# Moving four of the adaLN vectors from TensorE to VectorE, spread over four feed-forwards

## The chip, the core and the metric

One core of one Trainium2 chip runs the whole program in one launch. The time is device microseconds of that core, the median of three runs. A profile is one more execution; the rows below come from it.

## The reference, cut to what matters

Two blocks of layers run one after the other on 256 tokens of width 1024, beside 256 context tokens. Every layer is conditioned: a vector `c` (and another one for the context) is passed through Silu and multiplied by a weight matrix, and the product, plus a bias, is cut into vectors of 1024 that shift, scale and gate what the layer does.

```python
silu_c, silu_cc = silu(c), silu(c_ctx)
for i in range(2):                                  # first block
    mod_lat = (silu_c  @ mod_w[i] + mod_b[i])       # 9 vectors of 1024
    mod_ctx = (silu_cc @ mod_w[i] + mod_b[i])       # used by layer 0 alone
    ...
for i in range(2):                                  # second block
    sh1, sc1, g1, sh2, sc2, g2 = split(silu_c2 @ mod_w2[i] + mod_b2[i], 6)
    csh1, csc1, ... = split(silu_cc2 @ mod_w2[i] + mod_b2[i], 6)   # layer 0: the first two are used
    ...
```

There are 30 such vectors, each a product with a 1024 x 1024 piece of weights (4 MB in fp32). Vectors 0 to 4 of the first layer and 0 and 1 of the second block's first layer are wanted for both the tokens (keys `l00`..., `r00`...) and the context (`c0`..., `d0`...); all others for the tokens alone.

## The kernel before, in words

Everything is fp32 in feature-major tiles. A weight tile of 128 x 1024 is loaded raw (`wraw`, 512 KB, 3 buffers), cast by ScalarE to a high part (`wh`, L287) and split by VectorE into a low part (`wl`, L288; 6 buffers of each), and PE does three products for every pair (`mm3`).

The program runs: filters for the last mixer (`hyena_filters`), the joint feed-forward of tokens and context (`ffn_two`, 69.5 to 461 us of the span), attention (to 640), the feed-forwards `half_ffn(0,1)` and `half_ffn(1,0)`, a Fourier mixer, `half_ffn(1,1)`, the recurrent mixers (`ab_mixer`), the feed-forward `w130`, the Hyena mixer, the feed-forward `w131`. `ffn_two` has two halves; each makes 11 blocks of the up-projection (48 matmuls of 512 columns, a gate of ScalarE and VectorE) and then 8 pieces of the down-projection (33 matmuls).

The vectors are made in the background, in two ways. `mod_param` (L154) is PE's: for each of four `k` it loads a `modw` tile of 1 MB and multiplies it with the conditioning columns, 4 matmuls of 32 columns (8 instructions in the trace), for both rows at once; then ScalarE copies, PE transposes four times, VectorE adds the bias. That is five steps for a vector. `mod_vector` (L189) is VectorE's: for each of eight `c` it loads a `modx` tile of 512 KB (3 buffers) and reduces it against the broadcast row `crow` (L205). With two keys, each step has two more reductions of half the width for the second row (L201 to L204); no vector takes that path before. `VEC` (L63) says which vectors are VectorE's: 23 of 30, all those with one key. PE has seven.

Two generators, `fill` (PE's) and `fillv` (VectorE's), walk through the vectors in order; `pump(n)` and `pump_v(n)` trace their next `n` steps at a place in the program. `ffn_two` asks for `fillers[half]` steps of PE and `fillers[2]` of VectorE behind a block, and `fillers[3]` of VectorE behind a piece of the down-projection; the other feed-forwards take theirs from `self.ff`. `need(keys)` (L259) pumps until the keys are there. A scheduler then orders the instructions of each engine: of those that are ready by its reckoning, the earliest in the program goes first, so a step can run well ahead of its place in the text. Engines and queues work through that order strictly. Both ways take their tiles from one pool, `modp`, on `mstack`; SP's queue issues the loads of weights, `modw` and `modx`; POOL's queue loads `crow`.

In the filters 13 steps of PE's generator are asked for, which makes two vectors and three of the four products of the third.

```python
VEC = {"mw0": (5,6,7,8), "mw1": tuple(range(9)), "nw0": (2,3,4,5), "nw1": tuple(range(6))}
...
                self.pump(fillers[half])
                if j < HB - 1:
                    self.pump_v(fillers[2])
```

Of the kernel before, what the change touches and what calls it, by code (L numbers as in the profile page):

```python
# [19 lines left out]
KC = D // P  # L20
# [39 lines left out]
    return np.ascontiguousarray(w.reshape(2, 4, P, n, T).transpose(3, 0, 2, 1, 4))  # L60


VEC = {"mw0": (5,6,7,8), "mw1": tuple(range(9)), "nw0": (2,3,4,5), "nw1": tuple(range(6))}  # L63


def mod_tiles(w, vec):

    n = w.shape[1] // D
    t = w.reshape(KC, P, n, D).transpose(2, 0, 1, 3).copy()
    for j in vec:  # L70
        t[j] = w[:, j * D:j * D + D].T.reshape(KC, P, D)
    return t
# [6 lines left out]
class Gen:  # L79
    def __init__(self, tc, a, o):  # L80
        self.tc = tc
        self.nc = tc.nc
        self.a = a
        self.o = o
        self.n = 0
        self.hold, self.busy = False, set()
        self.ff = ((0,0,1,2),(0,0,1,2))
        self.gaps = (1,2,2)
        self.bg = []

# [139 lines left out]
    def filler(self, vec):  # L230
        for n, i, j, keys in self.mods():
            if (j in VEC[f"{n}w{i}"]) != vec:
                continue
# [23 lines left out]
            next(self.fillv, None)  # L257

    def need(self, *keys):  # L259
        while any(k not in self.prm for k in keys):  # L260
            self.pump(1)
            self.pump_v(1)


    def split(self, raw, shape, tag, pool=None, bufs=None):
# [306 lines left out]
            for x, *_ in todo:  # L572
                nc.scalar.activation(out=x[:, c, :], in_=x[:, c, :], func=AF.Copy, scale=ALPHA)

    def ffn_two(self, wi, wo, H, ahead, first, done, pool, fillers=(1,1,1,2)):

        hh, hl = lambda c: H[0][:, :, c, :], lambda c: H[1][:, :, c, :]
        for half in range(2):
            dh = pool.tile([P, HB, 2, T], F32R, tag="dh", name=self.nm("dh"), bufs=1)
            dl = pool.tile([P, HB, 2, T], F32R, tag="dl", name=self.nm("dl"), bufs=1)  # L580
            for j in range(HB):
                blk = ahead.pop() if ahead else [self.weights(wi[half * HB + j, x]) for x in range(2)]
                (pa, pg), = self.up_group([blk], hh, hl, 2 * T)
                self.glu(pa, pg, dh[:, j], dl[:, j], [P, 2, T], pool)
# [3 lines that stand above are left out]
            for f in range(KC):  # L588
                ps = self.po.tile([P, 2, T], F32, tag="out", name=self.nm("dn"))
                for c0 in (0, 8):  # L590
                    n = min(8, HB - c0)
                    wh, wl = self.weights(wo[f, :, half * HB + c0:half * HB + c0 + n, :])
                    for j in range(n):
                        self.mm3(ps, wh[:, j, :], wl[:, j, :], dh[:, c0 + j], dl[:, c0 + j],
                                 c0 + j == 0, c0 + j == HB - 1)
                (done if half else first)(f, ps)
                self.pump_v(fillers[3])


    def rope(self, dst, src, pool):  # L600
# [1149 lines left out]
    def build(self):  # L1750
        nc, tc, a, prm = self.nc, self.tc, self.a, self.prm
        pool = lambda n: tc.tile_pool(name=n, bufs=1, reuse_waits="tile")
        self.cols = self.cp.tile(list(a["cols"].shape), F32, tag="cols", name="cols")
        i = 0
# [8 lines left out]
        H = [h[:, :, 0:KC * T].rearrange("p n (c t) -> p n c t", c=KC) for h in Hr]  # L1763
# [5 lines left out]
        def post(l, j, X, s, sc, sh, out, alpha, tag="a"):  # L1769
            g, b = LG(l, j)  # L1770
            mod = None
            if sc is not None:
                self.need(sc, sh)
                mod = self.affine(g, b, sc, sh, tag)
            self.layer_norm(X, s, g, b, mod, out and out[0], out and out[1], alpha)
# [6 lines left out]
        def into(gate, n, l, sc, sh):  # L1782


            self.need(gate, sc, sh)
            s = self.acc_begin(False)
            r = []

            def done(f, ps):
                self.gated(X, prm[gate], s, f, ps)  # L1790
                if f == 1:
                    r.append(self.raw_begin(*R0, *self.affine(NW(n, l), None, sc, sh, "a")))
                    self.raw_chunk(r[0], X, 0)
                if f:
                    self.raw_chunk(r[0], X, f)

            def end():
                self.rms_norm(X, s, r[0].g2, r[0].sh, *H1, raw=r[0])
                return r[0]
            return done, end  # L1800
# [12 lines left out]
        ahead = []  # L1813
        with pool("hf") as p:
# [5 lines left out]
                    ahead.append([self.weights(a["wi00"][0, x]) for x in range(2)])  # L1820
            self.hyena_filters(kf, H, X, hook, p)

        with pool("f0") as p:
            while "c1" not in prm:
                self.pump(1)
            self.modulate([(X, "l01", "l00", *H0), (Xc, "c1", "c0", *H1)])
            sl, sc = self.acc_begin(True), self.acc_begin(True)

            def first(f, ps):
                self.need("l02", "c2")  # L1830
                for x, k, i in ((X, "l02", 0), (Xc, "c2", 1)):
                    nc.vector.scalar_tensor_tensor(out=x[:, f, :], in0=ps[:, i], scalar=prm[k][:, f:f + 1],
                                                   in1=x[:, f, :], op0=ALU.mult, op1=ALU.add)

            def second(f, ps):
                self.gated(Xc, prm["c2"], sc, f, ps[:, 1])
                self.gated(X, prm["l02"], sl, f, ps[:, 0])
            self.ffn_two(a["wi00"], a["wo00"], H, ahead, first, second, p)
            post(0, 0, Xc, sc, "c4", "c3", H1, None, "c")
            post(0, 0, X, sl, "l04", "l03", H0, ALPHA)  # L1840
# [42 lines left out]
        done, end = into("r02", "norm2", 0, "r04", "r03")  # L1883
        self.project(a["ab_wo"], *H1, done, early)
        raw = end()
        done, end = into("r05", "norm1", 1, "r11", "r10")
# [4 lines left out]
        done, end = into("r12", "norm2", 1, "r14", "r13")  # L1891
# [142 lines left out]
def host_inputs(v):  # L2034
# [7 lines left out]
    for i in range(2):  # L2042
        r[f"mw{i}"], r[f"nw{i}"] = mod_tiles(f("mod_w")[i], VEC[f"mw{i}"]), mod_tiles(f("mod_w_2")[i], VEC[f"nw{i}"])
        for k in range(2):
# [36 lines left out]
```

## Time and profile before

| | |
|---|---|
| median of the runs | 2132.93 us (2126.7 to 2133.91) |
| the profiled execution | 2130.68 us, span 2128.9 us |
| PE busy | 2023.3 us, 95% of the span |
| VectorE (DVE) busy | 1437.3 us, 68% |
| ScalarE (ACT) busy | 958.9 us, 45% |
| mean granted TensorE clock | 0.967 |
| HBM read | 400.78 MB, 191 GB/s over the span |

PE's busy time counts overlapping matmuls and weight loads as work and is no measure of how close PE is to its peak. The start of one matmul to the start of the next is the better measure of its pace. In the first fifth of the span the DMA engines move over 300 GB/s; after that less.

### The profile page before, as it was taken

How to read it: one execution, taken by the hardware profiler on the slowest of the kernel's cores; microseconds unless marked ns; L12 is line 12 of the kernel's file. 1: busy time of each engine (PE TensorE's matmuls, PEld its weight loads, DVE VectorE, ACT ScalarE, POOL GpSimd, SP SyncE). 2: the span in 40 equal slices, each digit the busy share in tenths (PEclk: the TensorE clock that was granted, in tenths of full speed). 3: DMA queues.
4: the chain of work that ended last, by engine and by line, in shares of the span. 5: the costliest groups of instructions: out<-in, count | busy, mean ns of one | idle time of the engine just before them, and what ended most of it. 6: DMA issues, size and time to landing. Idle time of an engine off the chain costs nothing.

```text
span 2128.9 us, 39134 instructions
## 1 busy us (share of the span) xinstructions
PE 2023.3 (95%) x15750; PEld 1848.4 (87%) x15750; DVE 1437.3 (68%) x2654; ACT 958.9 (45%) x1651; POOL 203.2 (10%) x240
## 2 busy tenths in 40 slices
PE   7999999977699999999999999989989999999998
PEld 3677877767579999999999997978879998999998
DVE  6766876899966555655565646686788757887553
ACT  3622222235656445544554436344354545445442
POOL 1000000150020001001120021211020001001001
PEclk9999999988899999999999998999989999999999
DMA  9988998886524664666346553222158865525663
GB/s 322 341 314 307 328 323 311 287 291 222 163 70 149 186 186 144 198 191 201 114 131 194 163 158 92 70 67 81 52 179 296 261 190 184 168 87 174 192 185 107
DMA packets 115885, 408.56 MB, mean 192 GB/s; under 512 B 13492, under 2 KB 16244, under 8 KB 115320
## 3 DMA queue, kind: packets, MB, share of 16 engines
q1 hardware_dynamic: 111480, 391.86, 56.4%
q0 software_dynamic: 4224, 14.21, 2.0%
q8 instruction: 123, 2.02, 0.4%
q14 instruction: 58, 0.48, 0.1%
HBM read 400.78 MB, written 5.24 MB: 191 GB/s over the span
## 4 chain that ended last, share of the span: by engine, by line
PE 67%; issue 18%; DVE 9%; DMA 3%; ACT 2%; POOL 1%; SPq 0%; POOLq 0%; DVEq 0%; ACTq 0%
PE up L293 30%; PE dn L293 14%; PE pfm L293 3%; PE pj L293 3%; PE ptm L293 3%; PE phu L293 2%; DVE modx L205 2%; DVE wl L288 2%; PE phs L293 1%; PE st L293 1%; PE phy L293 1%; PE phk L293 1%; ACT wh L287 1%; PE pu L293 1%; PE psk L293 1%
## 5 line engine op out<-in xcount | busy, mean ns | idle before, releaser
L288 DVE TENSOR_TENSOR wl<-wraw,wh 128x1024 fp32r<-128x1024 f32 (+1 forms) x511 | 611.4, 1198 | 397.4 <-ACT wh L287 396.6
L293 PE MATMUL up<-H,wh 128*128 128x256 f32 (+2 forms) x4224 | 858.2, 302 | 3.2 <-ACT H L499 3.2
L287 ACT CAST wh<-wraw 128x1024 fp32r<-128x1024 f32 (+1 forms) x511 | 517.7, 1014 | 713.3 <-PE up L293 334.5
L293 PEld LDWEIGHTS up<-H,wh 128*128 128x128 f32 x4224 | 679.8, 190 | 45.4 <-ACT silu L331 13.4
L293 PE MATMUL up<-H,wl 128*128 128x256 f32 (+2 forms) x2112 | 636.1, 301 | 2.8 <-DVE wl L288 2.8
L293 PEld LDWEIGHTS up<-H,wl 128*128 128x128 f32 x2112 | 405.9, 192 | 19.4 <-DVE wl L288 3.0
L293 PE MATMUL dn<-dl,wh 128*128 128x256 f32 (+1 forms) x1056 | 317.5, 301 | 0.6 <-DVE dl L335 0.6
L293 PE MATMUL dn<-dh,wh 128*128 128x256 f32 (+1 forms) x1056 | 317.7, 301 | 0.0
L293 PE MATMUL dn<-dh,wl 128*128 128x256 f32 (+1 forms) x1056 | 317.4, 301 | 0.0
L205 DVE CUSTOM_DVE_ANT_0 modx<-modx,crow 128x1024 f32<-128x1024 f32 x184 | 229.9, 1268 | 92.6 <-DMA modx<-i_mw 79.8
L293 PEld LDWEIGHTS dn<-dh,wh 128*128 128x128 f32 x1056 | 199.0, 188 | 8.8 <-issue 0.8
L293 PEld LDWEIGHTS dn<-dl,wh 128*128 128x128 f32 x1056 | 198.9, 188 | 8.7 <-DVE dl L335 1.1
L293 PEld LDWEIGHTS dn<-dh,wl 128*128 128x128 f32 x1056 | 199.0, 188 | 7.6
L293 PE MATMUL pj<-H,wh 128*128 128x256 f32 x480 | 86.5, 281 | 0.4 <-ACT H L473 0.3
L412 POOL TENSOR_TENSOR accQ<-accQ,sq 128x256 f32<-128x256 f32 x55 | 73.2, 1331 | 88.7 <-ACT sq L402 87.2
L334 ACT CAST dh<-gluh 128x256 fp32r<-128x256 f32 (+1 forms) x128 | 56.4, 443 | 47.6 <-DVE gluh L333 46.8
L293 PE MATMUL phu<-H,wh 128*128 128x256 f32 (+1 forms) x384 | 73.2, 288 | 3.4 <-ACT H L542 1.4
L293 PE MATMUL pfm<-H,wh 128*128 128x256 f32 (+1 forms) x288 | 74.0, 339 | 2.4 <-ACT t L1325 1.3
L293 PEld LDWEIGHTS pj<-H,wh 128*128 128x128 f32 x480 | 74.1, 188 | 1.3 <-ACT H L473 0.5
L293 PE MATMUL ptm<-wh,H 128*128 128x256 f32 x384 | 72.7, 291 | 0.0
L293 PE MATMUL pj<-H,wl 128*128 128x256 f32 x240 | 67.6, 282 | 1.8 <-DVE wl L288 1.8
L293 PEld LDWEIGHTS phu<-H,wh 128*128 128x128 f32 x384 | 60.9, 193 | 4.9 <-ACT H L542 1.8
(477 smaller groups left out, 2620.3 us busy)
## 6 DMA issues: line engine op xcount, KB each, us to landing
wraw<-i_wi SPq DMA_DIRECT2D x176, 512.0 KB, 4.5
wraw<-i_w SPq DMA_DIRECT2D x120, 512.0 KB, 4.2
modx<-i_mw SPq DMA_DIRECT2D x104, 512.0 KB, 5.8
modx<-i_nw SPq DMA_DIRECT2D x80, 512.0 KB, 4.8
wraw<-i_wo SPq DMA_DIRECT2D x64, 512.0 KB, 4.3
modw<-i_mw SPq DMA_DIRECT2D x20, 1024.0 KB, 8.0
wraw<-i_hy_in SPq DMA_DIRECT2D x24, 512.0 KB, 4.5
wraw<-i_wo SPq DMA_DIRECT2D x24, 384.0 KB, 3.8
```

Source lines behind the costliest of these rows:

```text
L205: nc.vector.tensor_tensor_reduce(out=ws[c - 1], in0=ws[c - 1], in1=rows[0], scale=1.0, scalar=0.0, op0=ALU.mult, op1=ALU.add, accum_out=ts ...
L287: nc.scalar.copy(out=hi[:, :f], in_=raw[:, :f])
L288: nc.vector.tensor_tensor(out=lo[:, :f], in0=raw[:, :f], in1=hi[:, :f].bitcast(F32), op=ALU.subtract)
L293: return self.nc.tensor.matmul(out, lhsT=l, rhs=r, start=start, stop=stop, skip_group_check=True, **kw)
L334: nc.scalar.copy(out=dh, in_=h)
L412: nc.gpsimd.tensor_tensor(out=s.Q, in0=s.Q, in1=sq, op=ALU.add)
```

## The change

`VEC` gives VectorE vectors 3 and 4 of the first layer and vectors 0 and 1 of the second block's first layer as well; all four have two keys. PE keeps vectors 0, 1 and 2 of the first layer. VectorE's steps rise from 184 to 216, PE's products fall from 28 to 12. Ahead of the joint feed-forward the program finishes PE's third vector, closes `modp` and opens it again, so that PE's 16 KB of `modw` buffers in each partition are given up and the rows `crow` are loaded anew. `ffn_two` asks for no PE steps, for 4 VectorE steps behind a block (1 before) and 3 behind a piece of the down-projection (2 before), none behind the last two pieces. The three feed-forwards of the first block ask for 1.3 steps a block (28 for 22). `need` pumps only the generator to which the missing key belongs.

```diff
-VEC = {"mw0": (5,6,7,8), "mw1": tuple(range(9)), "nw0": (2,3,4,5), "nw1": tuple(range(6))}
+VEC = {"mw0": (3,4,5,6,7,8), "mw1": tuple(range(9)), "nw0": tuple(range(6)), "nw1": tuple(range(6))}
...
-        self.ff = ((0,0,1,2),(0,0,1,2))
+        self.ff = ((0,0,1.3,2),(0,0,1,2))
...
     def need(self, *keys):
-        while any(k not in self.prm for k in keys):
-            self.pump(1)
-            self.pump_v(1)
+        for k in keys:
+            vec = any(k in ks and j in VEC[f"{n}w{i}"] for n, i, j, ks in self.mods())
+            while k not in self.prm:
+                self.pump_v(1) if vec else self.pump(1)
...
-    def ffn_two(self, wi, wo, H, ahead, first, done, pool, fillers=(1,1,1,2)):
+    def ffn_two(self, wi, wo, H, ahead, first, done, pool, fillers=(0,0,4,3)):
...
-                self.pump_v(fillers[3])
+                if half == 0 or f < KC - 2:
+                    self.pump_v(fillers[3])
...
+        self.need("c0", "c1", "c2")
+        self.mstack.close()
+        self.open_m()
         with pool("f0") as p:
-            while "c1" not in prm:
-                self.pump(1)
...
             def first(f, ps):
-                self.need("l02", "c2")
```

## Rows read from the trace of the kernel before

**Rows 1.** Busy times by stage: us, then PE, PEld, DVE, ACT, POOL; clock, DMA share, GB/s.
```profile
258.00:385.00 127.00, 127.00 (x579) 96.18 (x577) 88.75 (x154) 31.28 (x43) 0.00 (x0) 1.00 0.87 312
461.00:640.00 179.00, 136.42 (x944) 115.44 (x944) 152.00 (x379) 99.41 (x201) 20.33 (x22) 0.85 0.51 163
...
1595.00:1713.00 118.00, 117.97 (x988) 117.97 (x989) 90.36 (x134) 58.59 (x88) 0.00 (x0) 0.99 0.82 269
```
**Rows 2.** Groups by shape, 69.5 to 461 us: VectorE's reductions and PE's products.
```profile
L205 DVE CUSTOM_DVE_ANT_0 modx<-modx,crow 128x1024 f32<-128x1024 f32 x128 | 162.0, 1289 | 84.4 <-DMA modx<-i_mw 79.8 <-ACT crow L221 3.6 <-DMA modx<-i_nw 0.5
...
L293 PE MATMUL mod<-modw,cond 128*32 128x512 f32 x136 | 18.1, 605 | 0.0
```
**Rows 3.** Waits, 69.5 to 461 us: total us, times, longest.
```profile
ACT wh L287 <- PE up L293: 152.3, 18, 9.4
DVE modx L205 <- DMA modx<-i_mw: 79.8, 29, 5.7
```
**Rows 4.** Timeline of PE in the first block: start, us.
```profile
69.31 0.63 PE L293 MATMUL up<-H,wh 128*128 128x512 f32 x2
...
70.00 0.63 PE L293 MATMUL up<-H,wh 128*128 128x512 f32 x2
```
**Rows 5.** Timeline of ScalarE: the Silu at the end of three blocks.
```profile
153.33 0.59 ACT L331 ACTIVATE silu<-up 128x512 f32<-128x512 f32 x1
...
164.86 0.59 ACT L331 ACTIVATE silu<-up 128x512 f32<-128x512 f32 x1
...
177.14 0.59 ACT L331 ACTIVATE silu<-up 128x512 f32<-128x512 f32 x1
```
**Rows 6.** Timeline of VectorE, a reduction and the split behind it.
```profile
406.15 1.22 DVE L205 CUSTOM_DVE_ANT_0 modx<-modx,crow 128x1024 f32<-128x1024 f32 x1
...
407.30 1.22 DVE L288 TENSOR_TENSOR wl<-wraw,wh 128x1024 fp32r<-128x1024 f32 x1
```
**Rows 7.** Timeline of VectorE in the attention: two reductions of 512.
```profile
591.90 0.69 DVE L673 CUSTOM_DVE_ANT_0 sc<-pss,band 128x512 f32<-128x512 f32 x1
...
592.51 0.69 DVE L673 CUSTOM_DVE_ANT_0 sc<-pss,band 128x512 f32<-128x512 f32 x1
```
**Rows 8.** The tiles modw and modx: issues on SP's queue, ns min/median/max, first and last start.
```profile
L163 SPq DMA_DIRECT2D modw<-i_nw x8: 378/382/387, 191.4 to 360.6; - x8
...
L198 SPq DMA_DIRECT2D modx<-i_mw x104: 327/328/1052, 65.8 to 390.0; - x104
```
**Rows 9.** Timeline of VectorE: the first reduction; the second block's splits.
```profile
75.32 1.23 DVE L205 CUSTOM_DVE_ANT_0 modx<-modx,crow 128x1024 f32<-128x1024 f32 x1 [3.02 <-DMA modx<-i_mw]
...
78.93 2.52 DVE L288 TENSOR_TENSOR wl<-wraw,wh 128x1024 fp32r<-128x1024 f32 x2 [0.22 <-ACT wh L287]
```
**Rows 10.** Busy times and granted clock at the start of the attention.
```profile
493.00:496.00 3.00, 3.00 (x8) 2.32 (x8) 3.00 (x9) 2.32 (x5) 0.00 (x0) 0.50 0.94 370
```
**Rows 11.** Groups of VectorE by shape, 421 to 458 us.
```profile
L205 DVE CUSTOM_DVE_ANT_0 modx<-modx,crow 128x1024 f32<-128x1024 f32 x14 | 23.5, 1716 | 0.0
```
**Rows 12.** Timeline of PE behind the last down-projection.
```profile
464.19 1.02 PE L293 MATMUL st<-onem,Xc 128*128 128x1 f32 x4 [3.89 <-DVE Xc L548]
```
**Rows 13.** The tile modx by stretch: us, VectorE busy and count; clock, DMA share, GB/s.
```profile
397.00:461.00 64.00, 35.70 (x24) 1.00 0.87 295
...
520.00:640.00 120.00, 18.81 (x16) 0.91 0.42 135
640.00:835.00 195.00, 0.00 (x0) 0.98 0.59 177
...
1600.00:1713.00 113.00, 23.06 (x19) 1.00 0.83 273
```
**Rows 14.** Busy times in the attention behind the last reduction.
```profile
590.00:613.00 23.00, 20.12 (x138) 13.54 (x136) 15.03 (x46) 16.62 (x43) 0.00 (x0) 0.93 0.00 1
```
**Rows 15.** The chain behind the recurrent mixers: two updates of X.
```profile
1565.88 0.47 DVE X L548
...
1569.51 0.40 DVE X L548
```

## The prediction

> **What bounds the kernel now.** I read the busy times by stage first, then groups, waits and the timeline. The change acts in the joint feed-forward, from 69.5 to 461 us. There PE is busy without a gap at full clock, in the second up-projection for 127.00 of 127 us, while VectorE fills 88.75; from 461 to 640, in the attention, PE has gaps and VectorE is busy 152 of 179 us [rows 1]. So PE sets the pace up to 461 and VectorE is close behind; after it VectorE is nearest to the bound.
>
> Next the groups of that stretch: the matmuls on 32 columns for the vectors (mod), and 128 reductions (modx) at 1289 ns [rows 2]. The program text asks for 52 reduction steps in this stage; 128 ran. So steps are pulled forward from later feed-forwards into whatever time is free: the order of the program is a priority, not a place. The list of waits says that ScalarE's casts wait 152.3 us for PE to release a weight buffer, so the splits run as far ahead as the buffers let them, and that VectorE waits 79.8 us for modx loads without PE noticing [rows 3].
>
> **PE's relief.** Two pairs of matmuls of the up-projection follow each other by 0.69 us with one matmul between, so 0.231 us each and 48 x 0.231 = 11.1 us for a block [rows 4]. The Silu of the blocks starts at 153.33, 164.86 and 177.14: a block with four transposes takes 11.53 us, one with a product of a vector 12.28 [rows 5]. One product costs 12.28 - 11.1 = 1.17 us of PE, a set of transposes 0.43. Of 17 products in this stage (136 instructions by 8) [rows 2] 16 go (four vectors by four) and four sets of transposes: 16 x 1.17 + 4 x 0.43 = **-20.5 us**, all of it on PE, which is the bound. The ends are 0, if VectorE or the loads take over, and 20.5.
>
> **What moves to VectorE.** Four vectors of eight steps, all with two results, one for each conditioning row. A step has a 1024-wide reduction, 1.15 us from start to start [rows 6], and two 512-wide ones. No 512-wide modx ran; the nearest is the 512-wide reduction of the attention, 0.61 us from start to start, its other source in PSUM [rows 7]. So 1.15 + 2 x 0.61 = 2.37 us a step; 32 steps are 76 us of VectorE, against 20.5 us of PE. Below 0.58 (half the 1.15) and above 0.69 (its whole duration) I see no reason to go: 2.31 to 2.53.
>
> The bytes are the same, 16 loads of 1 MB for 32 of 512 KB. SP's queue issues 32 x 0.33 for 16 x 0.38 us [rows 8], 4.5 us more over 370; it waits for buffers most of that time, so I put nothing. In the trace loads of 512 KB are the rule already, and the last down-projection, which has no 1 MB loads, moved its weights and 24 steps in 64 us, at 0.87 of the DMA engines' time [rows 13]. The Trainium skill, page "DMA: Bandwidth & Descriptors", section "Rules for kernel authors", speaks against it: it wants 1 MiB in each transfer for full bandwidth. [...]
>
> **Early delay.** The first two vectors in VectorE's order (3 and 4 of the first layer) are of the two-result kind, though their results are wanted only at 460. Four steps are now asked for behind each block and so stand ahead of the splits of the next block. VectorE's load for a block is then 4 x 2.37 + 2 splits of 1.2 [rows 6] + 2 instructions of 0.61 for the gate, put at the 512-wide price above, = 13.1 us, and PE takes 11.1. Before, the first reduction ran at 75.32 and the second block's splits ended at 81.4 [rows 9]. With the pool closed and opened again, the rows loaded again and PE's third vector finished first, I put the first step at 82 (an estimate between 75 and 90). Before the fourth block's splits stand 12 steps, three gates and the splits: 82 + 28.4 + 3.7 + 2.4 = 116.5, while PE wants them at 81.4 + 2 x 11.1 = 103.6: 12.9 us late, and 2.0 more for the next block. Splits that slip in while a load is on its way take some of it off; a rest of that size also costs PE its clock: after its idle time from 459 on PE was granted 0.50 still at 493 to 496 [rows 10]. I take **+13 us**. The ends are 0 (all splits slip in) and +20 (none does, loads late, 5 us at half clock).
>
> **Late delay.** The next two-result vectors are steps 121 to 136. Before, the 128 steps up to 461 came out even; without the 1 MB loads step 121 comes at about the end of the second up-projection. So 16 two-result steps lie in the last down-projection, beside POOL's sums. There a reduction takes 1716 ns instead of 1.22 us, a factor of 1.40 [rows 6, 11], and VectorE ends 3.89 us behind PE [rows 12]. Before, 24 reductions lay there [rows 13]: 24 x 1.72 = 41 us. Now 16 x 2.37 x 1.40 = 53 us, 12 more on a full engine; if only the wide reduction is slowed, 16 x (1.15 x 1.40 + 1.22) = 45 and 4 more. The Trainium skill, "GPSIMD Engine Reference", section "Specifications", has VectorE contend with POOL in instructions with two SBUF inputs; the halves are such, so by that page it would be +12. I take **+6 us**, the splits being some blocks ahead; ends 0 and +12.
>
> **The rest of the work.** 216 steps instead of 184, 140 or so done at 461 instead of 128, so some 75 are left instead of 32 before the mixers, and 24 less after them. The attention took in 32, the last 16 of them after 520, and from 640 to 835 there is none [rows 13]: the supply had run out. Now it goes on. From 590 to 613 VectorE has 8 of 23 us free [rows 14]; at the pace before, 16 in 120 us or denser, five to eight more steps of 1.15 us come in there and in the norm at 640, part of them on the chain: **+5 us**, ends 0 (all in gaps) and +12 (each on the chain, and waits for loads of about 4 us). In the three feed-forwards behind, 30 steps fit beside a PE-bound up-projection: 19 steps between 1600 and 1713 left PE full, 117.97 of 118 us [rows 1, 13]; I put +1 for the start, ends 0 and 3. The closing of the pool itself moves the third vector's last product ahead of the modulation, 1 MB in front of the first blocks' weights: **+1**, ends -2 and +4. The extra memory is used by nothing.
>
> Behind the mixers nothing is left to reduce. The chain there runs through VectorE, and the updates of X come 3.63 us apart with reductions and a row's Silu between them [rows 15], where PE needs 24 matmuls of half the columns of an up-projection's, 24 x 0.116 = 2.8 us [rows 4]; six updates at 0.8 are 4.8, which I round down for what the weights hold up: **-4 us**, ends 0 and -6. The wait on the running vector ahead of the mixers costs nothing, before or after: it had long run.
>
> **Sum.** -20.5 + 13 + 6 + 5 + 1 + 1 - 4 = +1.5 us against the profiled execution's 2130.7 (span 2128.9 and 1.8 around it), which lies 2.2 below the median 2132.9. For the median: 2134.4, said as 2134. A change under 0.3%, 6.4 us, can't be told from none here.
>
> **Rivals.** *The relief wins.* If the splits keep slipping in during the first blocks, as they did before when all reductions were of lower priority, the early and late delays are some 4 and 2 us: -20.5 + 4 + 2 + 3 + 1 - 4 = -15, 2118. For it: VectorE's 79.8 us of waiting for modx loads are free time in which PE missed nothing [rows 3]. Against it: the free time lies inside an in-order queue, and the steps now stand first. *VectorE becomes the bound.* The place is the queue of VectorE between 82 and 130 and again from 400 to 461: if no split slips in and POOL slows the halves too, +20 + 12 + 6 + 1 + 1 - 20.5 - 3 = +16, 2149. It decides when the delay in the first four blocks is over 15 us. For it: 13.1 us of load against 11.1 a block; against it: buffers of three blocks. *It doesn't do what it says.* Since steps are pulled forward anyway, the new counts in the feed-forwards may move hardly anything, and only PE's four vectors count; then the two-result steps are gap-fillers and it ends near the first rival, 2116. [...]
>
> **Numbers.** Forecast 0.35; relief wins, with the case of idle counts, 0.30; VectorE bound 0.32; transfers 0.03. The forecast's own range is 2127 to 2139, the bounds of "same" about the median. 8 times in 10: from 2113, the relief with a lower price in the attention, to 2156, VectorE bound with a dearer attention. Faster 0.30, same 0.35, slower 0.35.
>
> **What would show it.** Right: no mod matmul after about 80 us; blocks of 11.1 us; PE idle for 10 us or more between 100 and 135, released by wl; reductions at 3 us a step in the last down-projection; modx instructions between 590 and 835; none after 1550. Wrong: no PE wait in the first four blocks (then it is faster by 10 to 20), or a wait on wraw loads, or the up-projections of the later feed-forwards longer than 128 us.

## The result, and the profile after

The changed kernel takes 2157.52 us (median of four runs, 2154.83 to 2160.77) against 2130.13 for the kernel before beside it (2126.7 to 2133.91): a ratio of 1.0124, 95% interval 1.0108 to 1.0140. That is 23 us above the forecast of 2134 and just above the range. The profiled span is 2156.5 us.

Where the 27 us arise is read from PE's timeline: the start of the first matmul of each stage. The table gives the kernel before in us and how much later each kernel gets there; the runs are explained below. Each column is one profiled execution, and that can lie off the median of its runs: by -4.5 us for before_slot, and by +9.4 us for two_moved, which is not in the table.

| stage starts | before | after | own_scratch | loads_alone | finish_first | before_slot | slot_4late |
|---|---|---|---|---|---|---|---|
| joint feed-forward | 63.7 | +12.6 | +11.9 | +13.5 | +15.1 | +0.9 | -0.2 |
| its second block | 81.0 | +9.3 | +8.5 | +10.3 | +15.7 | +4.7 | -0.2 |
| first down-projection | 202.3 | +17.1 | -1.8 | +18.1 | +14.5 | +8.8 | -0.2 |
| second down-projection | 396.5 | +9.0 | -7.7 | +11.1 | +13.0 | +8.8 | -0.2 |
| its last matmul | 458.9 | +16.2 | +5.3 | +16.4 | +17.6 | +7.7 | -1.3 |
| feed-forward (0,1) | 641.8 | -1.6 | +16.9 | -2.3 | +19.2 | -12.5 | -21.6 |
| feed-forward (1,0) | 838.5 | +23.1 | +28.6 | +0.9 | +20.2 | -4.3 | -21.6 |
| feed-forward (1,1) | 1086.2 | +34.4 | +29.9 | +3.1 | +21.5 | -5.3 | -10.0 |
| feed-forward w131 | 1930.1 | +28.3 | +27.0 | -0.5 | +17.9 | -14.1 | -18.2 |
| last matmul of it | 2118.2 | +27.2 | +25.8 | -1.7 | +17.9 | -15.3 | -19.3 |

In the column "after" the loss has four places: 9 to 13 us before the second block, 16 us within the first half (less 8 of relief), 7 us in the second down-projection, and 36 us between 640 and 1060. The attention is 17.8 us faster. The 36 us are 11.8 in the up-projection of (0,1), 12.9 in its down-projection and the norm behind, 2.5 in the up-projection of (1,0), and 8.8 from the start of its down-projection on.

The view of [rows 13], over the stages of the kernel after, shows where the reductions went: VectorE's busy time on the tile modx and the number of its instructions; then clock, DMA share, GB/s.
```profile
461.00:640.00 179.00, 0.00 (x0) 0.88 0.27 82
640.00:865.00 225.00, 80.66 (x78) 0.93 0.79 271
865.00:1062.00 197.00, 54.66 (x44) 0.98 0.84 283
1600.00:1720.00 120.00, 0.00 (x0) 0.97 0.62 189
```
No reduction runs in the attention any more; 94 of the 216 steps run in the feed-forwards (0,1) and (1,0), where the kernel before had none. Exactly 122 steps ran before the attention, as many as the program text asks for there: nothing is pulled forward past that point.

What PE waits for, in order of time (PE's timeline, start, duration, and in brackets the idle time before and its releaser):
```profile
71.24 1.94 PE L294 MATMUL mod<-modw,cond 128*32 128x512 f32 x8 [4.32 <-DMA modw<-i_mw]
...
114.89 0.80 PE L294 MATMUL up<-H,wl 128*128 128x512 f32 x1 [5.95 <-DVE wl L289]
...
144.24 0.79 PE L294 MATMUL up<-H,wl 128*128 128x512 f32 x1 [4.54 <-DVE wl L289]
...
418.28 0.80 PE L294 MATMUL dn<-dh,wh 128*128 128x512 f32 x1 [5.55 <-ACT dh L335]
...
852.15 1.01 PE L294 MATMUL st<-onem,X 128*128 128x1 f32 x4 [5.16 <-DVE X L549]
...
1002.18 0.58 PE L294 MATMUL dn<-dh,wh 128*128 128x256 f32 x1 [4.05 <-ACT dh L335]
```
The first is the third vector's last product, now ahead of the first block. Behind it stand the copies of ScalarE and the additions of VectorE, and behind those the modulation:
```profile
75.09 0.17 DVE L183 TENSOR_TENSOR m_l<-modt,cols 128x8 f32<-128x8 f32 x1 [13.43 <-PE modt L297]
```
The next two are the early delay. VectorE's timeline in front of the first of them: a step takes 1.15 + 2 x 0.61, from 97.09 to 99.46, as priced, and the split that PE wants, at 113.62, comes behind six of them, with one other split in between.
```profile
97.09 1.23 DVE L205 CUSTOM_DVE_ANT_0 modx<-modx,crow 128x1024 f32<-128x1024 f32 x1
...
98.23 0.69 DVE L203 CUSTOM_DVE_ANT_0 junk<-modx,crow 128x512 bf16<-128x512 f32 x1
...
98.85 0.69 DVE L203 CUSTOM_DVE_ANT_0 junk<-modx,crow 128x512 bf16<-128x512 f32 x1
...
99.46 1.22 DVE L205 CUSTOM_DVE_ANT_0 modx<-modx,crow 128x1024 f32<-128x1024 f32 x1
...
113.62 1.22 DVE L289 TENSOR_TENSOR wl<-wraw,wh 128x1024 fp32r<-128x1024 f32 x1
```
The wait at 418 is a row. The second block's row `crow` takes the buffer of the first block's, so it can be loaded only when that one has been read for the last time; ScalarE then stands at the row's Silu, with the last block's Silu and cast behind, and VectorE, which has that block's gate, stands at a reduction that needs the row (ScalarE's timeline, then the window of all engines with the granted clock, which is 0.50 of full speed there, the lower of its two levels, 1.2 GHz):
```profile
411.63 1.06 ACT L221 ACTIVATE crow<-crow 128x1024 f32<-128x1024 f32 x1 [3.77 <-DMA crow<-i_crow]
...
413.53 0.59 ACT L332 ACTIVATE silu<-up 128x512 f32<-128x512 f32 x1
```
```profile
418.00:421.00 3.00, 2.72 (x6) 2.11 (x7) 2.53 (x5) 1.37 (x3) 0.00 (x0) 0.50 0.89 273
```
The fifth is the norm between (0,1) and (1,0), 19.1 us long where it was 7.3. On VectorE the last two updates of X are 8.8 us apart, with reductions that wait for their loads in between, and PE comes back at a granted clock of 0.50:
```profile
842.78 0.48 DVE L549 SCALAR_TENSOR_TENSOR X<-dn,m_l,X 128x256 f32<-128x256 f32 x1
844.53 1.23 DVE L205 CUSTOM_DVE_ANT_0 modx<-modx,crow 128x1024 f32<-128x1024 f32 x1 [1.26 <-DMA modx<-i_nw]
...
848.07 1.23 DVE L205 CUSTOM_DVE_ANT_0 modx<-modx,crow 128x1024 f32<-128x1024 f32 x1 [0.66 <-DMA modx<-i_nw]
...
851.62 0.48 DVE L549 SCALAR_TENSOR_TENSOR X<-dn,m_l,X 128x256 f32<-128x256 f32 x1
```
```profile
852.00:862.00 10.00, 4.51 (x18) 4.05 (x19) 5.83 (x14) 2.48 (x5) 0.71 (x1) 0.50 0.80 280
```
The sixth is the start of the down-projection of (1,0), 8.2 us longer than before. VectorE multiplies the last block's gate (`gluh`) at 1001.16, behind a reduction that had waited for its load:
```profile
1000.01 1.23 DVE L205 CUSTOM_DVE_ANT_0 modx<-modx,crow 128x1024 f32<-128x1024 f32 x1 [2.59 <-DMA modx<-i_nw]
```
In the list of waits of 640 to 865 us transfers come to the front:
```profile
ACT wh L288 <- DMA wraw<-i_wi: 54.8, 34, 4.8
ACT wh L288 <- DMA wraw<-i_wo: 31.4, 21, 3.3
...
DVE modx L205 <- DMA modx<-i_nw: 14.3, 11, 2.5
```
From that list one would say that loads bind these feed-forwards. A raw buffer, however, is loaded again only when VectorE has split it, so a late VectorE looks like a late load. The run loads_alone tells them apart.

### The profile page after: what moved, and what is told of

It reads as the page before. It is cut to its first block, busy times and chain, and to the rows that moved or that the text cites. A ratio compares the mean times of both kernels' runs of the same rounds, so it can differ in the third digit from the quotient of the medians.

```text
span 2156.5 us, 38994 instructions
## 1 busy us (share of the span) xinstructions
PE 2020.2 (94%) x15606; PEld 1852.3 (86%) x15606; DVE 1509.3 (70%) x2841; ACT 957.8 (44%) x1643; POOL 192.4 (9%) x241
## 4 chain that ended last, share of the span: by engine, by line
PE 51%; issue 19%; DMA 11%; DVE 10%; ACT 4%; POOL 1%; SPq 0%; POOLq 0%; DVEq 0%; ACTq 0%
PE up L294 19%; PE dn L294 10%; DVE wl L289 4%; DMA modx<-i_nw 3%; PE pj L294 3%; DMA wraw<-i_wi 3%; PE pfm L294 3%; PE ptm L294 3%; DMA wraw<-i_wo 2%; PE phu L294 2%; ACT wh L288 2%; DVE modx L205 1%; PE phy L294 1%; PE phs L294 1%; PE bc L294 1%
## 5 line engine op out<-in xcount | busy, mean ns | idle before, releaser
L294 PE MATMUL up<-H,wl 128*128 128x256 f32 (+2 forms) x2112 | 641.1, 304 | 18.3 <-DVE wl L289 18.1
L294 PE MATMUL dn<-dh,wh 128*128 128x256 f32 (+1 forms) x1056 | 319.2, 302 | 10.2 <-ACT dh L335 9.6
L205 DVE CUSTOM_DVE_ANT_0 modx<-modx,crow 128x1024 f32<-128x1024 f32 x216 | 264.3, 1234 | 84.4 <-DMA modx<-i_mw 45.9
L294 PEld LDWEIGHTS dn<-dh,wh 128*128 128x128 f32 x1056 | 200.4, 190 | 19.2 <-ACT dh L335 10.2
L413 POOL TENSOR_TENSOR accQ<-accQ,sq 128x256 f32<-128x256 f32 x55 | 64.0, 1165 | 89.4 <-ACT sq L403 88.0
L334 DVE TENSOR_TENSOR gluh<-up,silu 128x256 f32<-128x256 f32 (+1 forms) x128 | 59.2, 465 | 11.1 <-ACT silu L332 11.1
```

The lines of the kernel that those rows point to most:

```text
L205: nc.vector.tensor_tensor_reduce(out=ws[c - 1], in0=ws[c - 1], in1=rows[0], scale=1.0, scalar=0.0, op0=ALU.mult, op1=ALU.add, accum_out=ts ...
L294: return self.nc.tensor.matmul(out, lhsT=l, rhs=r, start=start, stop=stop, skip_group_check=True, **kw)
L334: nc.vector.tensor_tensor(out=h, in0=pa, in1=s, op=ALU.mult)
L413: nc.gpsimd.tensor_tensor(out=s.Q, in0=s.Q, in1=sq, op=ALU.add)
```

## The experiments

All medians are against runs of the kernel before on the same chip (2129.7 to 2130.5).

**own_scratch.** Why does nothing run ahead? The scratch `junk` of the two-result steps shares the tag of the norms' tiles, whose three slots are given in program order. The edit:
```diff
-  junk = self.lp.tile([P, T], F32, tag="h32", ..., bufs=3).bitcast(BF16)
+  junk = self.lp.tile([P, T], F32, tag="vjunk", ..., bufs=1).bitcast(BF16)
```


> The kernel after, with one edit: the scratch of the two-result reductions has a tile of its own instead of one of the three slots that it shares with the norms. Theory (slots): in the kernel after the steps from the 122nd on could not run ahead, because their scratch takes its turn behind the tiles of the attention's norms. Then here 20 or more reductions run between 461 and 640 us (none in the kernel after), the feed-forwards (0,1) and (1,0) get shorter, and the time is 10 to 25 us below the kernel after: 2133 to 2148. Rival (the attention has no room, or loads hold the steps back): still none between 461 and 640, and 2157 within 4.

Measured: 2156.57 us, 1.0122 (1.0106 to 1.0137). The mechanism is there, the gain is not. The reductions are back in the attention:
```profile
465.00:640.00 175.00, 59.23 (x51) 0.84 0.57 184
640.00:860.00 220.00, 52.79 (x43) 0.95 0.79 263
860.00:1060.00 200.00, 0.00 (x0) 0.98 0.59 183
```
The early delay is gone altogether (table: +11.9 to -1.8 in the first half; every block from the second on takes 11.1 us), so in the kernel after it too came with the shared slots: in this run's VectorE timeline the splits come between the reductions. (The edit also leaves one buffer where there were three; which of the two the early blocks owe it to, no run separates.) But the last down-projection now loses 13 us, the attention 11.6, the feed-forward (0,1) 11.7. What one place saves, another pays.

**both.** own_scratch with `fillers=(0,0,1,2)` in the joint feed-forward.

> The scratch of its own, and the joint feed-forward asks for 1 step a block and 2 a piece as in the kernel before, not 4 and 3. Theory (slots, and early delay by priority): no reduction in the feed-forwards (0,1) and (1,0), which then last as in the kernel before (126.8 us of up-projection, 7.3 us for the norm between them); the waits of 9.7 and 6.2 us in the first five blocks shrink; the attention pays some 15 to 30 for its steps. 2130 to 2148. Rival (the steps are bound wherever they lie): 2150 to 2160.

Measured: 2166.62, 1.0175 (1.0159 to 1.0192): slower still and above both ranges, so the time forecast by the theory is refuted, though (0,1) and (1,0) are within 1.3 us of the kernel before. 43 steps went behind the mixers, into w130, whose up-projection became 21 us longer.

**before_closed.** The kernel before with `self.need("c0", "c1", "c2"); self.mstack.close(); self.open_m()` and the new `need` alone.

> The kernel before, with only the closing: PE's third vector is finished and the pool closed and opened again ahead of the joint feed-forward; PE keeps its seven vectors. Theory (the closing is dear): PE stands behind the third vector's last load and VectorE's in-order queue behind its two additions, so the first block starts 9 to 13 us later, and that stays to the end: 2139 to 2143. As the prediction had it, -2 to +4: 2128 to 2134.

Measured: 2140.40, 1.0051 (1.0034 to 1.0067). As the theory: +10.

**loads_alone.** The loads of the second block's vectors stay, their reductions read 8 columns, the 512-wide ones too; so these vectors are not computed.
```diff
+  f = slice(0, D if keys[0][0] == "l" else 8)
-  ... in0=ws[c - 1], in1=rows[0], ...
+  ... in0=ws[c - 1][:, f], in1=rows[0][:, f], ...
```


> The kernel after, but for the vectors of the second block the reductions read 8 columns of each weight tile instead of all; the loads stay whole, so those vectors are not computed. Theory (transfers bind the feed-forwards (0,1) and (1,0)): their up-projections stay at 136 to 140 us, and the time within 8 us of the kernel after: 2149 to 2158. Rival (VectorE's queue binds them): up-projections of 127 us, and 2120 to 2132.

Measured: 2131.05, 1.0008 (0.9991 to 1.0024): 26.5 us less than the kernel after. The rival was right; transfers do not bind here. The up-projection of (0,1), all engines (PE, PEld, VectorE, ScalarE, POOL; clock, DMA share, GB/s), first here, then in the kernel after, where it lasted until 778.9:
```profile
640.00:770.00 130.00, 130.00 (x1088) 130.00 (x1087) 84.19 (x251) 70.11 (x109) 0.00 (x0) 0.98 0.83 300
```
```profile
640.00:780.00 140.00, 133.37 (x1066) 131.85 (x1067) 124.23 (x238) 69.20 (x106) 0.00 (x0) 0.96 0.75 255
```
More bytes per us, and PE without a gap, once VectorE has 84 of 130 us to do and not 124 of 140.

**before_slot.** The reverse of own_scratch: the kernel before, whose one-result steps are now held by the norms' slots.
```diff
+  acc = ts[0][:, c - 1:c]
+  if keys[0][0] == "r":
+      acc = self.lp.tile([P, T], F32, tag="h32", ..., bufs=3)[:, 0:1]
   nc.vector.tensor_tensor_reduce(..., accum_out=acc)
+  if keys[0][0] == "r":
+      nc.vector.tensor_copy(out=ts[0][:, c - 1:c], in_=acc)
...
-  fillers=(1,1,1,2)
+  fillers=(1,1,4,3)
```


> The kernel before (no two-result step, pool open, PE's seven vectors), but the steps of the second block's vectors hold one of the norms' three scratch slots, as the two-result steps of the kernel after do, and the joint feed-forward asks for 4 and 3 steps, so that those steps run where the program has them: in the feed-forwards (0,1) and (1,0), none in the attention. Theory (slots decide the place; VectorE is the bound there only with the wide two-result load): attention 15 to 18 us shorter, the two feed-forwards 0 to 8 longer, 2116 to 2128. Rival (the feed-forwards pay for any step, as in the kernel after): 20 us or more there, 2132 to 2145.

Measured: 2120.29, 0.9954 (0.9940 to 0.9969): faster than both kernels, as the theory. 31 one-result steps in the up-projection of (0,1) cost 1.1 us, and the attention without them is 20 us shorter. The down-projection behind, with 3 steps, lost 7.1: in its first piece PE waits 3.65 us for the last block's cast. And the joint feed-forward, which asks for four steps a block here, lost 8.8 us in its first half, though no step there holds a slot: ScalarE's casts for the second block wait 3.04 and 3.35 us for weight loads.

**two_moved.** Vectors 3 and 4 of the first layer alone on VectorE, PE keeps the other two; scratch in the slots of the squares, the second row in the feed-forward's own pool, so that nothing has to be closed.

> The kernel before with vectors 3 and 4 of the first layer alone moved to VectorE, their scratch in the slots of the squares, the pool left open, the old fillers. Theory: PE's relief is 8 products and two sets of transposes, 10.2 us; no wait in the first five blocks; VectorE's 38 us come out of its 80 us of waiting for loads, with 3 to 6 given back in the last down-projection and the attention: 2121 to 2128. Rival (VectorE is full as soon as any two-result step is added): 2130 to 2140.

Measured: 2143.18, 1.0063 (1.0046 to 1.0080). The rival, and worse. In the profiled execution (2152.6 us) the first two blocks lose 6 us, as ScalarE's Silu of the second row waits 5.32 us for its load and the casts stand behind; PE gains 9 us in the second half (the table's way of counting: +6.3 to -2.9); the second down-projection gives 9.5 back, and the up-projection of w130, where 34 steps run instead of 20, takes 11 more.

**one_result.** own_scratch, with one result for vectors 0 and 1 of the second block's first layer.

> As the run with the scratch of its own (2156.6 us), but vectors 0 and 1 of the second block's first layer get only their first result, which is used for both; the second is not computed: 16 steps of 1.15 instead of 2.37 us. Theory (VectorE's extra 19.5 us are what the last down-projection, the attention and the feed-forward (0,1) pay for): 12 to 20 us less, 2137 to 2145. Rival (the number of steps and their loads decide): 2150 to 2158.

Measured: 2140.12, 1.0051 (1.0036 to 1.0066), 16.4 less than own_scratch, as the theory: of the 19.5 us taken off VectorE, a share of 0.84 comes off the end.

**two_moved_slot.** two_moved with the edit of before_slot.

> Vectors 3 and 4 of the first layer on VectorE, pool open, and the second block's steps held in the feed-forwards by the norms' slots, as above. Theory: the gains of the two runs above add up, 2110 to 2122. Rival (the feed-forwards pay for the steps): 2128 to 2140.

Measured: 2139.63, 1.0051 (1.0034 to 1.0068), the rival. The gains did not add up: with 4 two-result steps asked for behind each block the first half lost 19 us.

**slot_4late.** before_slot, with `self.pump_v(fillers[2] if half else 1)` in the joint feed-forward and `if m < NB - 3:` ahead of the other feed-forwards' steps.

> As the run with the kernel before and the second block's steps held by the norms' slots (2120.3 us), but the joint feed-forward asks for 1 step a block in its first half (4 only in the second), and the other feed-forwards ask for none behind their last three blocks. Theory: the 8.8 us that the first half lost come back, as do the 7 us at the start of the down-projection of (0,1), where the last block's gate stood behind steps that waited for loads; the steps spread over (0,1), (1,0) and (1,1): 2104 to 2113. Rival (the steps cost the same wherever they end up): 2117 to 2124.

Measured: 2113.96, 0.9914 (0.9891 to 0.9937), 1 us above the theory's range. The 8.8 us came back, and the start of the down-projection of (0,1) is clean; (1,0) now shows the same wait:
```profile
957.26 0.58 PE L298 MATMUL dn<-dh,wh 128*128 128x256 f32 x1 [4.35 <-ACT dh L339]
```

**closed_late.** before_closed with `self.need("c0", "c1"); self.pump(1)` ahead of the closing and `self.need("l02", "c2")` back behind the modulation.

> As the run with the early closing alone (2140.4 us), but of PE's third vector only the last product and its two copies stand ahead of the closing; its transposes and additions come behind the modulation. Theory (the closing costs because the modulation stands behind those additions in VectorE's queue): VectorE's wait of 13 us shrinks by 3 or more, 2132 to 2137. Rival (the load of the last product and the reloaded row are what costs): 2138 to 2143.

Measured: 2138.90, 1.0038 (1.0025 to 1.0051): the rival. The additions are not what costs. VectorE still waits 12.1 us, now at the clearing of the new pool's tile of conditioning columns, and ScalarE's copies of the product, which wait 6.75 us for PE, still stand ahead of the modulation's casts.

**two_slot_4late** and **all_4late.** The order of slot_4late, with two vectors moved, and with all four and the early closing.

> Vectors 3 and 4 of the first layer on VectorE as well, pool open, with the order of the run slot_4late. Theory (VectorE has room once the attention and the ends of the up-projections are kept free): PE's 10.2 us come on top, 2096 to 2106. Rival (VectorE's 38 us more take it back, as in the run that moved these two alone): 2110 to 2125.

> The kernel after, its four vectors on VectorE and the pool closed early, with that order: the scratch of the first layer's two-result steps in slots that are free, the second block's steps held by the norms' slots, 1 step a block in the first half, none behind the last three blocks of the other feed-forwards, the third vector's transposes behind the modulation. Theory (where the steps lie costs the kernel after most of its 27 us, the closing 10): 2118 to 2134. Rival (the four vectors are too much for VectorE in any order): 2140 to 2155.

Measured: 2133.04, 1.0003 (0.9988 to 1.0017), and 2144.11, 1.0062 (1.0036 to 1.0087). The first lies above both of its ranges, on the rival's side; the second is the rival. Beside slot_4late two more vectors on VectorE cost 19 us, four of them and the closing 30. In none of the orders tried did moving a vector pay.

**finish_first.** before_closed without `close` and `open_m`.

> The kernel before, with PE's third vector finished ahead of the joint feed-forward, as in the run with the early closing, but the pool neither closed nor opened again. Theory (the order costs: the modulation stands, on ScalarE and VectorE, behind the vector's copies and additions, and these wait for its last load): the first block starts 7 to 12 us later, 2137 to 2142. Rival (the closing costs: waits for the old tiles, rows and columns loaded again): 2128 to 2133.

Measured: 2146.77, 1.0077 (1.0060 to 1.0093): +17, above both ranges. So finishing the vector first is enough; closing is not needed for the loss. PE waits for the last 1 MB, ScalarE's copies for PE, the modulation's split for ScalarE (timelines of PE, ScalarE, VectorE):
```profile
74.03 1.94 PE L294 MATMUL mod<-modw,cond 128*32 128x512 f32 x8 [4.82 <-DMA modw<-i_mw]
```
```profile
76.03 0.65 ACT L173 COPY mods<-mod 128x256 f32<-128x256 f32 x2 [7.28 <-PE mod L294]
```
```profile
77.02 0.43 DVE L475 TENSOR_TENSOR H<-h,H 128x256 fp32r<-128x256 f32 x1 [13.21 <-ACT H L474]
```
Why it costs 7 us more than with the closing stays open.

**one_result_slot.** The kernel after, one result for the same two vectors, each step still in a slot of the norms.

> The kernel after, with vectors 0 and 1 of the second block's first layer computed for the first row alone (the second result is not computed), each step still in a slot of the norms, so that the steps lie where the kernel after has them. Theory (VectorE's time in the feed-forward (0,1), 19.5 us of second results, is what that one pays): its up-projection returns from 138.4 to 127 to 131 us, 12 to 20 off the end, 2138 to 2146. Rival (the number of steps and their loads): 2152 to 2160.

Measured: 2149.33, 1.0085 (1.0062 to 1.0107): between the two. The first half of the theory holds: the up-projection of (0,1) is 127 us again, PE full:
```profile
640.00:770.00 130.00, 130.00 (x1092) 129.99 (x1092) 110.31 (x193) 66.62 (x102) 0.00 (x0) 0.99 0.82 289
```
But the down-projection behind, with 18 steps, lost 8.6 (1.1 in the kernel after) and the norm, with 3, lost 8.1 (11.8 there). The second results fill VectorE in the up-projection; behind it one-result steps cost too, by where they stand in the queue.

**slot_8late.** slot_4late with `NB - 8` for `NB - 3`.

> As the run slot_4late (2114.0 us), but no step behind the last eight blocks of the other feed-forwards instead of three. Theory (8.7 us at the start of the down-projection of (1,0) come from steps around its last blocks): 2103 to 2110. Rival (what is taken out there is paid in the feed-forward behind the mixers): 2112 to 2118.

Measured: 2111.26, 0.9910 (0.9892 to 0.9928), the lowest median, 2.7 below slot_4late and in neither range; the runs of the two overlap (2107.25 to 2113.87, 2111.24 to 2115.53), so which is faster is not shown. The start of the down-projection of (1,0) is clean (1.3 us lost over it instead of 8.8); in the profiled execution the joint feed-forward lost 3 us on that of the other run, and 8 steps moved into w130, whose up-projection then took 2.8 us more than the kernel before's, instead of 6.6 less.

## Why the prediction was wrong, point by point

- **PE's relief**, -20.5: right. Blocks without a product take 11.1 us. From the first block to the second down-projection own_scratch goes from +11.9 to -7.7: 19.6 us. In the kernel after 16.3 of it show beside the waits.
- **A two-result step at 2.37 us**: right to the last digit.
- **Early delay**, +13: the third block takes 20.8 us and the fifth 17.3 instead of 11.1, so 9.7 + 6.2 = 15.9 us. Size and mechanism (splits behind steps) were right, but what puts the steps ahead was half seen: own_scratch asks for the same four steps a block and has no such wait, so here the edit of the scratch alone took it away. The number asked for can cost as well, as the first half of before_slot shows (8.8 us, gone in slot_4late with one step a block).
- **Late delay**, +6: 7.2, by another cause. Only two steps ran there; it was the reload of `crow` in front of the last gate. That the size came out is luck. Where two-result steps did run there, in own_scratch (12 of them, and 7 others), it was 13, just above the upper end of 12.
- **Attention**, +5: -17.8. The step failed at its root, "the order of the program is a priority, not a place". For a step that takes a slot shared with the program's own tiles, and for the steps behind it, it is a place.
- **Feed-forwards behind**, "30 steps fit beside a PE-bound up-projection", +1: 36. This is the term that decided. 94 steps came, not 30, the first 14 with two results. In (0,1) PE needs 126.9 / 22 = 5.8 us a block; VectorE has two splits of 1.15, a gate of 0.7 and 30 / 22 steps of 2.37: 6.2. Over the ten blocks or so that 14 steps fill, that is an estimated 4 to 5 us; 11.8 were lost, 5.9 of them in the fourth block, where PE waits 3.02 us for a split behind a reduction; so the average load is part of the cause, and the order in the queue another. With steps of 1.15 the load is 4.6; before_slot and one_result_slot ran that within 1.1 us of full pace, while own_scratch, with 34 such steps, lost 4.2. The other 24 us of the 36 are not a matter of that load: most of them are the norm behind (0,1) and the start of the down-projection of (1,0), where an update or a gate stands behind reductions that wait for loads. The evidence drawn on, 19 steps in w130, was of the cheap kind and too few, and the window from 1595 on left out the start: with its 20 steps that up-projection takes 133.1 us up to the down-projection, and 126.4 to 127.9 in the runs in which no step lies there.
- **The closing**, +1 within -2 to +4: 9.3. "1 MB in front of the first blocks' weights" counted the bytes; what counted was the order on ScalarE and VectorE, where the modulation of the first block stood behind work that waits for the vector's last load (before_closed +10.2 us, finish_first +17.1).
- **Behind the mixers**, -4: -7, with 24 steps gone from there. Up to the first matmul of w130 the kernel after loses 3 us more; then the up-projection of w130 is 6 us shorter, and 4 more are won behind it. That the shorter chain of updates of X brought this is not shown.

The sum by the terms as the profiled execution shows them: 9.3 + 15.9 - 7.6 (relief, first half) - 8.7 (second) + 7.2 - 17.8 + 36 - 7.2 = 27.1. So the step that failed is "30 steps fit beside a PE-bound up-projection", at +1: 36 us, because the slots held 94 steps there, at the price of two results or in front of a gate or an update. The closing, 9.3 us where +1 stood, is the second.

The rival "VectorE becomes the bound" was right in its engine (loads_alone) and in part of its place, the first blocks; most of the loss lies from 640 on, which it did not name. That transfers bind, to which the prediction gave a chance of 0.03 and which is the theory of loads_alone, is refuted for these feed-forwards: that run moved its 512 KB loads at 300 GB/s beside a PE without a gap. The Trainium skill, "DMA: Bandwidth & Descriptors", "Rules for kernel authors", asks for 1 MiB in each transfer; loads of half that size show no cost in these rows, and whether larger ones would move faster, no run tried.

## What to carry to other kernels

Before work is moved from a bound engine to one that seems free, count that engine's load in every stage in which the work may end up, at the price of the moved form, and not in the stage it was meant for. A background step runs ahead only as far as every tile that it takes comes free: scratch shared with foreground tiles ties it to its place, which can hurt (here, two-result steps before splits) or be used on purpose (one-result steps kept out of the attention and away from the last gate of an up-projection: slot_4late and slot_8late, 0.9% faster than the kernel before). A wait for a load may be a late consumer that frees the buffer late; shrink the consumer and keep the load, and see.

## What the runs showed of the hardware

Beside POOL's sums the 512-wide reductions lose time as well as the wide ones (own_scratch, last down-projection: VectorE's timeline, then POOL's; start, duration):
```profile
428.63 1.23 DVE L203 CUSTOM_DVE_ANT_0 junk<-modx,crow 128x512 bf16<-128x512 f32 x1
...
429.91 1.10 DVE L203 CUSTOM_DVE_ANT_0 junk<-modx,crow 128x512 bf16<-128x512 f32 x1
...
431.06 1.64 DVE L205 CUSTOM_DVE_ANT_0 modx<-modx,crow 128x1024 f32<-128x1024 f32 x1
...
432.63 0.68 DVE L203 CUSTOM_DVE_ANT_0 junk<-modx,crow 128x512 bf16<-128x512 f32 x1
```
```profile
428.25 1.07 POOL L413 TENSOR_TENSOR accQ<-accQ,sq 128x256 f32<-128x256 f32 x1
429.27 1.19 POOL L412 TENSOR_TENSOR accR<-accR,X 128x256 f32<-128x256 f32 x1
430.42 1.19 POOL L413 TENSOR_TENSOR accQ<-accQ,sq 128x256 f32<-128x256 f32 x1
```
The first two lie wholly beside the sums and take 1.23 and 1.10 us, the last, alone, 0.68: factors of 1.8 and 1.6, where the prediction had 1.40 from the mean of 14 wide ones, of which at least one ran alone (1210 to 1765 ns). The wide one shares only 0.55 us with the last sum, which ends at 431.61, and takes 1.64 instead of 1.22: it loses 0.42 us, as much as the second, which shares all of its 1.10. So in these rows the loss is not in proportion to the overlap. The Trainium skill, "GPSIMD Engine Reference", "Specifications", has VectorE contend with POOL in instructions with two SBUF inputs; the trace agrees, the halves included.
